# One 512-column matmul for both activation parts in the projections of a hybrid encoder trunk

## The chip, the cores and the metric

The kernel runs on one core of a Trainium2 chip. The metric is the device time of one execution in microseconds (us), given as the median of several runs; smaller is better. The engines are named as in the profile: PE is TensorE's matmul side, PEld its weight loads, DVE is VectorE, ACT is ScalarE, POOL is GpSimd and SP is SyncE, which issues the transfers.

## The reference

The reference is a two-layer encoder on 256 tokens of width 2048, in float32. Each layer normalises x, projects it to 6848 columns with one matrix, sends part of the columns through a recurrence in both directions over time (16 heads) and part through windowed attention (16 query heads, 4 key heads), gates both results, joins them and projects back to 2048 columns. Cut to what matters here:

```
for l in range(DEPTH):                                   # DEPTH = 2
    h = rms_norm(x, norm_g[l])
    proj = einsum('btd,dc->btc', h, w_in[l])             # 2048 -> 6848
    rw_in, g_rw, q, k_at, v_at, g_at = split(proj)
    rw_in = bidir_token_shift(rw_in, shift_mu[l])        # u + mu0*(prev-u) + mu1*(next-u)
    ...
    mix = concat([y_rw * silu(g_rw), y_at * silu(g_at)])
    x = x + einsum('btc,cd->btd', mix, w_out[l])         # 2048 -> 2048
return rms_norm(x, final_g)
```

The two large products, with `w_in` and `w_out`, are what the change touches.

## The kernel before, in words

**Precision by parts.** The matmuls of the projections read a rounded float32 form (`F32R`). To keep more of float32's accuracy each operand is split in a high part, the rounded value, and a low part, the rest. A product is then the sum of three matmuls: high weights by high activations, high weights by low activations, and low weights by high activations.

**Tiles and steps.** Activations lie transposed: 128 channels on the partitions, 16 such blocks, 256 tokens along the free dimension. A tile of an output is 128 columns of the projection by 256 tokens, accumulated in one PSUM tile `pm` over 16 steps of 128 input channels. One step (`gemm`, L292 to L294) is the three matmuls named above, each with its own load of 128x128 weights and 256 moving columns. Per layer there are 52 such input tiles: 42 are evacuated with a multiply by the norm `rb` (26 with the token shift, `shift_evac`, and 16 gates, `silu_evac`) and 10 are rotary (`rope_evac`). The output projection has 16 more (`queue_output`). The values of attention (`v_step`, L561 to L563) are the same three products with the activations as the stationary operand and 256 weight columns as the moving one, 32 steps a layer.

**Weights.** They stream in half tiles of 8 steps: one transfer of 512 KB to `raw` (three buffers), then `wsplit`, in two pieces of 512 columns: ACT writes `hi` (L222), DVE subtracts and writes `lo` (L224). `hi` and `lo` are separate tiles with two buffers each. The split of the next half tile is put into the program two steps before the present half tile ends (`PREFETCH`).

**Order.** PE runs in the order of the program (`manual_schedule` names PE alone). The order on DVE and ACT is set when the kernel is built, by a scheduler that goes by dependencies, priorities (`tc.high_priority`) and its own costs; instructions made with `PA` and `PV` keep program order among themselves. Each engine then works strictly through its list. A `Stream` holds the steps of all projections. `window` interleaves 64 steps, four tiles, with the pieces of the recurrence of several head pairs (`scan_p`, `scan_i`, `scan_b`, the yields of generators) in 14 slots, so that while ACT and DVE work on a piece of the recurrence, PE has steps to do. There are twelve such windows with recurrence work in each layer, then attention alone, then the 16 output tiles with nothing beside them. Once a window the recurrence takes a power on POOL (`yv`, L1000), between two instructions of DVE (L999 and the multiply into `ysq`).

**Evacuation.** When a tile's last matmul is done, DVE multiplies `pm` by `rb` into `u` or `g` (L434, L445), and ACT and DVE go on from there. Rotary tiles are copied out by ACT (L533). Output tiles are added to the residual by DVE (L624). `pm` has two buffers in `ps_main`, so PE can fill one tile while the other is evacuated. The split activations are `XH`, `XL` for the input and `MH`, `ML` for the output projection, each a buffer of 16 KB per partition in the pool `big`, which has four.

## Time and profile before

| | |
|---|---|
| time, median of 3 runs (lowest to highest) | 1187.89 us (1187.58 to 1188.18) |
| profiled execution, from the first to the last instruction | 1186.6 us |
| TensorE clock granted, mean | 0.995 |
| PE / PEld busy | 1160.9 us (98%) / 1082.7 us (91%) |
| DVE busy | 908.2 us (77%), 2017 instructions |
| ACT busy | 777.3 us (66%), 1955 instructions |
| matmuls | 16151 |
| moved to and from memory | 166.63 MB, mean 140 GB/s |

Rows of groups read: line, engine, operation, output <- inputs, shape, count; then the busy time in us and the mean of one in ns; then the idle time of the engine just before, and what ended it. In the timeline the first number is the start in us and the second what the instruction took. In the table by stage each engine has its busy time and, in brackets, its number of instructions; then come the granted clock of TensorE as a share, the share of the transfer engines and GB/s. Waits read: who waited for whom, total us, times, longest.

### The profile page before, as it was taken

The page shows a single profiled execution, that of the slowest core. Times are in us where ns is not written, and L with a number is a line of the kernel's source. Part 1 is how long each engine was busy: PE and PEld are TensorE (multiplying, and loading weights), DVE is VectorE, ACT ScalarE, POOL GpSimd, SP SyncE. Part 2 cuts the span into 40 slices and gives each one's busy share as a digit, 9 for nine tenths or more (in the row PEclk, how much of TensorE's full clock was granted, in tenths as well). Part 3 has the DMA queues.
Part 4 walks back from the last instruction along what each step waited for, and adds up shares of the span by engine and source line. Part 5 has one row for each costly group of instructions (what it writes and reads, how often), then busy time and mean ns, then how long its engine had stood idle before and what let it go on. Part 6 is the DMA issues. An engine that isn't in the chain of part 4 may idle for free.

```text
span 1186.6 us, 38095 instructions
## 1 busy us (share of the span) xinstructions
PE 1160.9 (98%) x16151; PEld 1082.7 (91%) x16151; DVE 908.2 (77%) x2017; ACT 777.3 (66%) x1955; POOL 18.7 (2%) x23
## 2 busy tenths in 40 slices
PE   8999999999999999999999999999999999999996
PEld 6988998999889989899999999999999998889996
DVE  6889878987877678766677988887887866786654
ACT  6666776777776666645555766876777666665553
POOL 0000000000000000000000000000000000000000
PEclk9999999999999999999999999999999999999998
DMA  7553333333323434477664443333323334345653
GB/s 257 164 170 123 109 107 116 108 98 115 109 94 122 136 117 142 134 234 236 210 184 165 134 131 114 95 113 117 122 83 109 122 124 132 114 145 190 213 185 123
DMA packets 60410, 166.63 MB, mean 140 GB/s; under 512 B 7728, under 2 KB 22736, under 8 KB 60240
## 3 DMA queue, kind: packets, MB, share of 16 engines
q1 hardware_dynamic: 60240, 164.21, 43.0%
q8 instruction: 126, 2.06, 0.7%
q14 instruction: 44, 0.36, 0.1%
HBM read 157.37 MB, written 4.19 MB: 136 GB/s over the span
## 4 chain that ended last, share of the span: by engine, by line
PE 74%; issue 15%; DVE 7%; ACT 2%; POOL 1%; DMA 1%; SPq 0%; DVEq 0%; POOLq 0%; ACTq 0%
PE pm L292 19%; PE pm L294 16%; PE pm L293 16%; PE pg L786 3%; DVE lo L224 2%; PE pcc L957 2%; PE py L987 2%; PE py L964 1%; PE pcc L980 1%; PE pq L899 1%; PE pcc L970 1%; PE pd L908 1%; PE pza L671 1%; POOL yv L1000 1%; PE pscr L1050 1%
## 5 line engine op out<-in xcount | busy, mean ns | idle before, releaser
L292 PE MATMUL pm<-XH,hi 128*128 128x256 f32 x1664 | 494.2, 297 | 3.9 <-ACT XH L184 1.6
L294 PE MATMUL pm<-XH,lo 128*128 128x256 f32 x1664 | 467.8, 281 | 5.9 <-DVE lo L224 5.8
L293 PE MATMUL pm<-XL,hi 128*128 128x256 f32 x1664 | 467.6, 281 | 0.8 <-DVE XL L185 0.6
L222 ACT ACTIVATE hi<-raw 128x512 fp32r<-128x512 f32 x560 | 328.2, 625 | 190.6 <-PE pm L293 91.8
L224 DVE TENSOR_TENSOR lo<-raw,hi 128x512 fp32r<-128x512 f32 x560 | 369.1, 686 | 102.5 <-ACT hi L222 95.2
L292 PEld LDWEIGHTS pm<-XH,hi 128*128 128x128 f32 x1664 | 313.4, 188 | 19.3 <-ACT XH L184 2.6
L294 PEld LDWEIGHTS pm<-XH,lo 128*128 128x128 f32 x1664 | 313.9, 189 | 8.3 <-DVE lo L224 8.3
L293 PEld LDWEIGHTS pm<-XL,hi 128*128 128x128 f32 x1664 | 314.1, 189 | 1.7 <-DVE XL L185 1.7
L292 PE MATMUL pm<-MH,hi 128*128 128x256 f32 x512 | 144.0, 281 | 0.0
L294 PE MATMUL pm<-MH,lo 128*128 128x256 f32 x512 | 143.8, 281 | 0.0
L293 PE MATMUL pm<-ML,hi 128*128 128x256 f32 x512 | 143.8, 281 | 0.0
L292 PEld LDWEIGHTS pm<-MH,hi 128*128 128x128 f32 x512 | 96.6, 189 | 0.8 <-issue 0.8
L293 PEld LDWEIGHTS pm<-ML,hi 128*128 128x128 f32 x512 | 96.6, 189 | 0.0
L294 PEld LDWEIGHTS pm<-MH,lo 128*128 128x128 f32 x512 | 96.6, 189 | 0.0
L910 DVE CAST_PREDICATED tv<-LV,pd 128x256 f16<-128x256 uint8 x80 | 34.2, 428 | 12.0 <-PE pd L908 11.4
L1065 ACT ACTIVATE mv<-mv,mx 128x257 f32<-128x257 f32 x64 | 31.9, 503 | 17.2 <-DVE mx L1062 17.2
L792 DVE TENSOR_TENSOR ge<-pg,C 128x1024 f32<-128x1024 f32 x32 | 38.8, 1219 | 2.3 <-PE pg L786 2.3
L975 ACT ACTIVATE suv<-pcc 64x128 f32<-64x128 f32 x128 | 34.3, 268 | 9.2 <-PE pcc L973 7.4
L959 ACT ACTIVATE rh<-pcc 128x128 f32<-128x128 f32 x64 | 17.5, 274 | 34.0 <-PE pcc L957 33.6
L902 ACT ACTIVATE QF<-pq 128x256 f16<-128x256 f32 x80 | 30.8, 384 | 12.5 <-PE pq L866 11.7
L786 PE MATMUL pg<-mv,bk 64*128 64x128 f32 x512 | 37.2, 285 | 0.3 <-DVE ge L792 0.3
L786 PEld LDWEIGHTS pg<-mv,bk 64*128 64x128 f32 x512 | 31.1, 187 | 2.4 <-DVE ge L792 0.4
(248 smaller groups left out, 1856.5 us busy)
## 6 DMA issues: line engine op xcount, KB each, us to landing
raw<-wi SPq DMA_DIRECT2D x207, 512.0 KB, 3.7
raw<-wo SPq DMA_DIRECT2D x64, 512.0 KB, 4.2
raw<-wv SPq DMA_DIRECT2D x8, 512.0 KB, 3.6
rrot<-u SPq DMA_DIRECT2D x80, 32.0 KB, 1.9
vg<-xT SPq DMA_DIRECT2D x16, 128.0 KB, 4.1
xd<-vg SPq DMA_DIRECT2D x16, 128.0 KB, 3.5
vg<-xd SPq DMA_DIRECT2D x16, 128.0 KB, 3.6
g<-dup SPq DMA_DIRECT2D x16, 97.0 KB
```

The lines of the kernel that those rows point to most:

```text
L222: A.activation(hi[:, q], raw[:, q], AF.Copy)
L224: V.tensor_tensor(lo[:, q], raw[:, q], hi[:, q].bitcast(F32), op=ALU.subtract)
L292: PE.matmul(pm, wh, rh[:, kk, :], start=(kk == 0), stop=False)
L293: PE.matmul(pm, wh, rl[:, kk, :], start=False, stop=False)
L294: PE.matmul(pm, wl, rh[:, kk, :], start=False, stop=(kk == 15))
L786: PE.matmul(pg[:, h, c * 128 : (c + 1) * 128], BK[half[h], d, c, 1 - h : 3 - h, :].rearrange("p s j -> p (s j)"), MV[half[h], d, c].rearra ...
L792: V.tensor_tensor(GEd(d), pg.rearrange("p h (c x) -> p h c x", c=NC), gm[d].unsqueeze(1).unsqueeze(1).to_broadcast([128, 2, NC, 128]), op= ...
L902: A.activation(t_sub(QF), flat4(pq[:, :, 0:128]), AF.Copy)
L910: V.copy_predicated(t_sub(TC), t_mask, flat4(pd[:, :, 0:128]))
L957: PE.matmul(pc[half[h], 0, d, :], GE[h][r, d, ci[d], 0, :], SUV[r, d, ci[d], h, :], start=True, stop=True)
L975: A.activation(here(h), pc[half[h], 1], AF.Copy)
L1065: A.activation(Sc[:, h, q, 0:257], Sc[:, h, q, 0:257], AF.Exp, scale=0.125, bias=mx[:, q : q + 1], accum_out=den[:, q : q + 1])
```

## The change

Both activation parts now lie beside each other in one buffer (`XP`, `MP`: 16 blocks, each of 256 high and 256 low columns), and both weight parts in one tile `hl`. A step has two matmuls: the high weights by 512 moving columns, both activation parts at once, into a PSUM tile of two halves; and the low weights by the 256 high columns into the first half. On a tile's last step the order of the two is turned round. The two halves, not yet one number, are added in the evacuation: in `joined` by a DVE `tensor_reduce` over pairs that are 256 elements apart, ahead of the multiply by `rb`; in the rotary tiles ACT copies the second half and DVE adds the first; in the output tiles a second DVE addition follows. `v_step` does the same with the two weight parts as 512 moving columns. The pool `big` has two buffers of twice the size.

```
-    big = pool("big", 4)
+    big = pool("big", 2)
...
+    def pairt(name):
+        hl = big.tile([128, NKT, 2, T], F32R, tag="big", name=name)
+        return hl, hl[:, :, 0], hl[:, :, 1]
...
     def wsplit(raw):
-        hi = wsp.tile([128, 1024], F32R, tag="hi", name="hi")
-        lo = wsp.tile([128, 1024], F32R, tag="lo", name="lo")
+        hl = wsp.tile([128, 2, 1024], F32R, tag="hl", name="hl")
+        hi, lo = hl[:, 0], hl[:, 1]
...
-        return hi, lo
+        return hi, lo, hl
...
-                    box.append(bank() if bank else ps_main.tile([128, T], F32, tag="m", name="pm"))
+                    box.append(bank() if bank else ps_main.tile([128, 2, T], F32, tag="m", name="pm"))
...
-                rh, rl = operands()
+                r = operands()
                 k = kk % 8
                 wh, wl = w[0][:, k * 128 : (k + 1) * 128], w[1][:, k * 128 : (k + 1) * 128]
-                PE.matmul(pm, wh, rh[:, kk, :], start=(kk == 0), stop=False)
-                PE.matmul(pm, wh, rl[:, kk, :], start=False, stop=False)
-                PE.matmul(pm, wl, rh[:, kk, :], start=False, stop=(kk == 15))
+
+                def high():
+                    PE.matmul(pm, wh, r[:, kk], start=(kk == 0), stop=(kk == 15), skip_group_check=True)
+
+                def low():
+                    PE.matmul(pm[:, 0], wl, r[:, kk, 0], start=False, stop=False, skip_group_check=True)
+
+                for part in (low, high) if kk == 15 else (high, low):
+                    part()
...
+        def joined(u, pm):
+            V.tensor_reduce(u, pm.rearrange("p s t -> p t s"), axis=AX.X, op=ALU.add)
+            V.tensor_tensor(u, u, L.norm.rb, op=ALU.mult)
...
-                V.tensor_tensor(u, pm, L.norm.rb, op=ALU.mult)
+                joined(u, pm)
...
-                V.tensor_tensor(g, pm, L.norm.rb, op=ALU.mult)
+                joined(g, pm)
...
-                A.activation(raw, pm, AF.Copy)
+                A.activation(raw, pm[:, 1], AF.Copy)
+                V.tensor_tensor(raw, pm[:, 0], raw, op=ALU.add)
...
-                wh, wl = (x[:, k * 256 : (k + 1) * 256] for x in w)
+                both = w[2][:, :, k * 256 : (k + 1) * 256]
                 tb = slice(b * 128, (b + 1) * 128)
-                PE.matmul(pvs[b], L.XH[:, kk, tb], wh, start=(kk == 0), stop=False)
-                PE.matmul(pvs[b], L.XH[:, kk, tb], wl, start=False, stop=False)
-                PE.matmul(pvs[b], L.XL[:, kk, tb], wh, start=False, stop=(kk == 15))
+                PE.matmul(pvs[b], L.XH[:, kk, tb], both, start=(kk == 0), stop=(kk == 15), skip_group_check=True)
+                PE.matmul(pvs[b][:, 0], L.XL[:, kk, tb], both[:, 0], start=False, stop=(kk == 15), skip_group_check=True)
...
-                A.activation(L.VA[:, 0, :], pvs[0], AF.Copy, scale=L.norm.rt[:, 0:1])
-                V.tensor_scalar(L.VA[:, 1, :], pvs[1], L.norm.rt[:, 1:2], None, op0=ALU.mult)
+                for b in range(2):
+                    A.activation(L.VA[:, b, :], pvs[b][:, 0], AF.Copy, scale=L.norm.rt[:, b : b + 1])
+                    V.scalar_tensor_tensor(
+                        L.VA[:, b, :], pvs[b][:, 1], L.norm.rt[:, b : b + 1], L.VA[:, b, :], op0=ALU.mult, op1=ALU.add
+                    )
...
-                V.tensor_tensor(x, pm, xs[0], op=ALU.add)
+                V.tensor_tensor(x, pm[:, 0], xs[0], op=ALU.add)
+                V.tensor_tensor(x, pm[:, 1], x, op=ALU.add)
```

The change moves instructions at three places. The first is PE's list at the first steps of the first tile, before (`XH`, `XL` are the activation parts, `hi`, `lo` the weight parts):

```order
L292 MATMUL pm<-XH,hi 128x256
L293 MATMUL pm<-XL,hi 128x256
L294 MATMUL pm<-XH,lo 128x256
L292 MATMUL pm<-XH,hi 128x256
L293 MATMUL pm<-XL,hi 128x256
L294 MATMUL pm<-XH,lo 128x256
```

and in the changed kernel at the end of the first tile and the start of the second (the line numbers have moved on):

```order
L299 MATMUL pm<-XP,hl 128x512
L302 MATMUL pm<-XP,hl 128x256
L299 MATMUL pm<-XP,hl 128x512
L302 MATMUL pm<-XP,hl 128x256 x2
L299 MATMUL pm<-XP,hl 128x512 x2
L302 MATMUL pm<-XP,hl 128x256
L299 MATMUL pm<-XP,hl 128x512
```

Three matmuls a step have become two; at the seam two of the short and two of the long follow each other. The second place is DVE's list around the power `yv` in a window of layer 1, before:

```order
L999 TENSOR_SCALAR yv<-yv 128x4
L237 TENSOR_TENSOR ysq<-py,yv 128x256
L224 TENSOR_TENSOR lo<-raw,hi 128x512 x2
L910 COPY_PREDICATED tv<-LV,pd 128x2x4x32
L237 TENSOR_TENSOR th<-lw,th 128x256
L445 TENSOR_TENSOR g<-pm,rb 128x256
L224 TENSOR_TENSOR lo<-raw,hi 128x512 x2
L447 SCALAR_TENSOR_TENSOR vg<-g 128x256
```

and in the changed kernel, where L229 writes the low weights, L930 is the former L910 and L443 and L444 are the reduce and the multiply:

```order
L1019 TENSOR_SCALAR yv<-yv 128x4
L453 SCALAR_TENSOR_TENSOR kr<-u,PR,kr 128x255
L242 TENSOR_TENSOR ysq<-py,yv 128x256
L229 TENSOR_TENSOR hl<-raw,hl 128x512
L930 COPY_PREDICATED tv<-LV,pd 128x2x4x32
L229 TENSOR_TENSOR hl<-raw,hl 128x512
L242 TENSOR_TENSOR th<-lw,th 128x256
L443 TENSOR_REDUCE g<-pm 128x256
L229 TENSOR_TENSOR hl<-raw,hl 128x512
L444 TENSOR_TENSOR g<-g,rb 128x256
L229 TENSOR_TENSOR hl<-raw,hl 128x512
```

The scheduler has put the last instruction of a token shift (L453) between the power's two DVE instructions, the copy into `tv` between the two low parts, and a low part between the reduce and its multiply. The third place is DVE's list in the output projection of layer 1, before:

```order
L624 TENSOR_TENSOR X_20063<-pm,vg 128x256
L224 TENSOR_TENSOR lo<-raw,hi 128x512 x2
L640 TENSOR_TENSOR acc<-acc,mf 128x256
L224 TENSOR_TENSOR lo<-raw,hi 128x512 x2
L624 TENSOR_TENSOR X_20063<-pm,vg 128x256
```

and changed:

```order
L643 TENSOR_TENSOR X_17932<-pm,vg 128x256
L644 TENSOR_TENSOR X_17932<-pm,X_17932 128x256
L229 TENSOR_TENSOR hl<-raw,hl 128x512 x2
L660 TENSOR_TENSOR acc<-acc,mf 128x256
L229 TENSOR_TENSOR hl<-raw,hl 128x512 x2
L643 TENSOR_TENSOR X_17932<-pm,vg 128x256
```

The order is the same but for the second addition behind the first.

More of the change, by code (lines that the diff above doesn't have):

```diff
@@ L479, in queue_inputs @@
         if l == 0:
-            inproj(0, lambda pm: S.later(29, lambda: xw_evac(pm)), raws=first_w, bank=lambda: wbank("pm")[:, 0:T])
+            inproj(0, lambda pm: S.later(29, lambda: xw_evac(pm)), raws=first_w, bank=lambda: wbank("pm").rearrange("p (s t) -> p s t", s=2))
             inproj(1, lambda pm: S.later(13, lambda: xa_evac(pm)))
@@ L556, in f @@
                 if not pvs:
-                    pvs.extend(ps_main.tile([128, T], F32, tag="m", name="pva") for _ in range(2))
+                    pvs.extend(ps_main.tile([128, 2, T], F32, tag="m", name="pva") for _ in range(2))
                 k = kk % 4
-                wh, wl = (x[:, k * 256 : (k + 1) * 256] for x in w)
+                both = w[2][:, :, k * 256 : (k + 1) * 256]
                 tb = slice(b * 128, (b + 1) * 128)
-                PE.matmul(pvs[b], L.XH[:, kk, tb], wh, start=(kk == 0), stop=False)
-                PE.matmul(pvs[b], L.XH[:, kk, tb], wl, start=False, stop=False)
-                PE.matmul(pvs[b], L.XL[:, kk, tb], wh, start=False, stop=(kk == 15))
+                PE.matmul(pvs[b], L.XH[:, kk, tb], both, start=(kk == 0), stop=(kk == 15), skip_group_check=True)
+                PE.matmul(pvs[b][:, 0], L.XL[:, kk, tb], both[:, 0], start=False, stop=(kk == 15), skip_group_check=True)
             return f
```

10 lines of the change are left out of this document (5 added, 5 removed).

## The prediction

> **What bounds the kernel now.** I read the page first: its busy rows and the engine line of the chain of waits.
>
> ```profile
> span 1186.6 us, 38095 instructions
> PE 1160.9 (98%) x16151; PEld 1082.7 (91%) x16151; DVE 908.2 (77%) x2017; ACT 777.3 (66%) x1955; POOL 18.7 (2%) x23
> ...
> PE 74%; issue 15%; DVE 7%; ACT 2%; POOL 1%; DMA 1%; SPq 0%; DVEq 0%; POOLq 0%; ACTq 0%
> ```
>
> TensorE (PE) ends almost every wait, and VectorE (DVE) is the only other engine with a share of the chain that matters. Since matmuls overlap, a busy PE says little about its pace. For that I read the table by stage: two full windows of layer 0's recurrence, two of layer 1's (each two POOL instructions long, since a window has one `yv` power), the two output projections, layer 0's attention, and then the two long stretches with recurrence work.
>
> ```profile
> core 0: us, PE busy (x) PEld busy (x) DVE busy (x) ACT busy (x) POOL busy (x), PEclk, DMA share, GB/s
> 189.85:272.82 82.97, 82.29 (x1502) 75.61 (x1502) 70.18 (x151) 60.08 (x162) 2.05 (x2) 1.00 0.34 108
> 770.34:852.70 82.36, 82.27 (x1502) 75.68 (x1501) 68.01 (x142) 59.81 (x162) 2.01 (x2) 1.00 0.34 109
> 504.30:595.20 90.90, 90.90 (x768) 90.90 (x767) 59.17 (x111) 47.26 (x95) 0.00 (x0) 1.00 0.72 227
> 1082.50:1173.40 90.90, 90.90 (x768) 90.90 (x767) 52.00 (x94) 47.72 (x93) 0.00 (x0) 1.00 0.59 186
> 440.00:504.30 64.30, 64.30 (x557) 58.52 (x553) 52.38 (x166) 43.63 (x120) 0.00 (x0) 1.00 0.45 144
> ...
> 51.00:440.00 389.00, 383.29 (x6433) 351.96 (x6433) 315.31 (x681) 271.73 (x711) 8.24 (x8) 1.00 0.36 116
> 632.00:1020.00 388.00, 384.72 (x6449) 353.89 (x6449) 310.20 (x662) 268.62 (x709) 8.06 (x8) 1.00 0.37 118
> ```
>
> The output projections are nothing but matmuls at full clock: 768 in 90.90 us is 118.4 ns each, 355.1 ns for the three of a step. The two layers' windows hold the same PE work (82.29 and 82.27 us), yet layer 0's take 41.49 us and layer 1's 41.18. DVE is busy 35.09 us of the one and 34.01 of the other. So DVE already leaks into the time: 1.08 us more of its work goes with 0.30 us more, 0.28 us per us.
>
> **TensorE.** These groups give the number of steps.
>
> ```profile
> L292 PE MATMUL pm<-XH,hi 128*128 128x256 f32 x1664 | 494.2, 297 | 3.9 <-ACT XH L184 1.6 <-ACT hi L222 1.4 <-DVE VA L571 0.7
> L292 PE MATMUL pm<-MH,hi 128*128 128x256 f32 x512 | 144.0, 281 | 0.0
> L561 PE MATMUL pva<-hi,XH 128*128 128x256 f32 x64 | 19.2, 300 | 0.0
> ```
>
> That is 1664 + 512 + 64 = 2240 steps. Each loses two matmuls of 256 columns and gets one of 512; the `lo` matmul stays at 118.4 ns. At the start some 30 steps wait for inputs (only 107 matmuls run in the first 24 us), so 2210 count.
>
> No f32 matmul of 512 columns is in the trace. From above, it costs two of the present: 236.8 ns, no gain. From below stand the f16 matmuls of the warm-up, whose last starts are 0.22 and 0.21 us apart at granted clock 1.00 (three overlapping views of the timeline, one row each, then the clock):
>
> ```profile
> 4.02 0.81 PE L1125 MATMUL warm<-QF 128*128 128x512 f16 x3
> 4.24 0.81 PE L1125 MATMUL warm<-QF 128*128 128x512 f16 x3
> 4.45 0.59 PE L1125 MATMUL warm<-QF 128*128 128x512 f16 x2
> ...
> 3.90:4.70 0.80, 0.80 (x6) 0.30 (x4) 0.63 (x1) 0.13 (x1) 0.00 (x0) 1.00 0.88 261
> ```
>
> So 215 ns for 512 columns, 0.42 ns a column, and 107.5 ns for 256: the present 118.4 carries 11 ns on top. Is that a fixed cost per matmul, or the weight load? The timeline shows the next load starting with each matmul, in lockstep with it:
>
> ```profile
> 1090.04 0.28 PE L292 MATMUL pm<-MH,hi 128*128 128x256 f32 x1
> 1090.04 0.19 PEld L293 LDWEIGHTS pm<-ML,hi 128*128 128x128 f32 x1
> 1090.15 0.28 PE L293 MATMUL pm<-ML,hi 128*128 128x256 f32 x1
> 1090.16 0.19 PEld L294 LDWEIGHTS pm<-MH,lo 128*128 128x128 f32 x1
> ```
>
> If the load sets the pace, the long matmul hides it and costs 215; if the 11 ns are fixed, 118.4 + 107.5 = 226. I take the middle, 221. A step is then 339 ns, 15.8 ns less: 2210 × 15.8 = **35 us off PE**. The ends are 0 (236.8) and, with 215 for the long one and 107.5 for the `lo` matmul too, 32.6 ns a step, 72 us.
>
> On the Trainium skill, TensorE: Matmul & The Clock Gate, section Back-to-back issue gap, gives N/2.4 + 2.5 ns, 109 ns for 256 columns and 216 for 512. The trace's 118.4 does not agree with the first; by the rule for both, a step would be 325 ns and the gain 30 ns a step, about 66 us.
>
> **VectorE.** The cost of an instruction is the distance of starts, since neighbours overlap (first rows of the timeline, then groups).
>
> ```profile
> 224.81 0.68 DVE L224 TENSOR_TENSOR lo<-raw,hi 128x512 fp32r<-128x512 f32 x1
> 225.41 0.68 DVE L237 TENSOR_TENSOR bk<-lw,ip 128x512 f32<-128x512 f32 x1
> ...
> 229.78 0.42 DVE L237 TENSOR_TENSOR lw<-lw 128x256 f32<-128x256 f32 x1
> 230.11 0.69 DVE L224 TENSOR_TENSOR lo<-raw,hi 128x512 fp32r<-128x512 f32 x1
> ...
> L434 DVE TENSOR_TENSOR u<-pm,rb 128x256 f32<-128x256 f32 x52 | 21.1, 408 | 10.0 <-PE pm L294 9.9
> L445 DVE TENSOR_TENSOR g<-pm,rb 128x256 f32<-128x256 f32 x32 | 13.4, 418 | 5.2 <-PE pm L294 5.2
> L792 DVE TENSOR_TENSOR ge<-pg,C 128x1024 f32<-128x1024 f32 x32 | 38.8, 1219 | 2.3 <-PE pg L786 2.3
> ```
>
> 512 elements cost 0.60 us, 256 cost 0.33, and a PSUM source costs no more (408 to 418 ns against 420 for `lw`). The multiply by `rb` remains in all 52 + 32 = 84 evacuations, so what is added is the reduce. It reads 512 elements and writes 256; from below, priced by its output, 0.33 us; from above, were a read that jumps 1 KB each time half as fast, the 1024 elements of L792 with the same overlap, 1.14. I take 0.60, the row with the same number of inputs. That is 84 × 0.60 = 50 us more DVE, with 20 additions for the rotary tiles and 32 for the output tiles (52 × 0.33 = 17 us) 67 us in all; `v_evac` adds two instructions per layer. The ACT copy of the rotary tiles stays, at half the tile.
>
> What hides it: a window has four evacuations, 2.4 us. DVE goes from 34.0 to 36.4 us in layer 1 and from 35.1 to 37.5 in layer 0, in windows that PE alone would shorten by 64 × 15.8 ns = 1.0 us, to 40.2 and 40.5. That is 91% and 93%. If this cover were gone, all 2.4 us would be on the path. At the slope above, 2.4 us more work and 1.0 us less room cost (2.4 + 1.0) × 0.28 = 0.95 us a window. The stretches with recurrence work, 389 + 388 us, are 18.8 windows: **18 us given back**. What is late then is `lo`: the reduce waits for PE as L434 does now, and behind it in DVE's queue stand the next `lo`, which PE's 256-column matmul needs, and `tv`, which the recurrence's matmuls need.
>
> Each attention stage (DVE 52.38 of 64.30 us) holds 8 tiles, by the order in the code six gates and two rotary: 6 × 0.60 + 2 × 0.33 = 4.3 us more, in 128 steps that are 2.0 us shorter. At the slope, 1.8 us each, 3.6. In the output projections DVE has 31 us free of 90.90, so 16 × 0.33 us is hidden; only the last tile's addition shows, 0.4 us at each end, 0.8.
>
> **Edits at nothing.** One `hl` tile for both weight parts comes free after its last matmul, where `hi` came free one earlier: ACT's `hi` starts up to 118 ns later, before work that is due a half tile (8 steps, 2.7 us) on. `v_step` needs `lo` with its first matmul, 8 loads in all. Two large buffers in place of four hold the same bytes in the same order. `pm` fills a bank but still has two buffers, and comes free with the reduce, 16 steps before it is wanted. SP's transfers stay the same.
>
> **The sum**, against the profiled 1186.6: −35 + 18 + 3.6 + 0.8 gives 1174.0. The median of the runs, 1187.89, is 1.3 above the span, so I add 1.3: **1175 us**.
>
> **Rivals.** (a) *The weight load was the pace and DVE finds room.* For it: the lockstep, and that some DVE waits are for PE and shrink; against it: DVE at over 90%. The long matmul costs 215, a step 333.4, 21.7 ns less: 48 us gained; with a third of the payback (7): 1187.9 − 48 + 7 = 1147. The page's 325 ns would take it to about 1135.
>
> (b) *The long matmul costs two short ones.* Nothing in the trace excludes it, though the f16 rows speak against it. PE gains nothing; DVE costs 2.4 × 0.28 × 18.8 = 13 us, and 3 us in attention and at the ends: 1204, slower. This side begins where the gain falls under some 17 us, at 8 ns a step, so from 229 ns for the long matmul.
>
> (c) *The reduce is slow and DVE becomes the bound.* At 1.14 us, four add 4.6 us: 38.6 and 39.7 us of work a window. These waits of one window of layer 1 (797 to 838 us) follow DVE's own results through POOL and ACT, and do not shrink:
>
> ```profile
> DVE ysq L237 <- POOL yv L1000: 1.2, 1, 1.2
> DVE t L237 <- ACT t L1009: 1.1, 1, 1.1
> ...
> DVE tt L894 <- ACT AB L237: 0.6, 1, 0.6
> ```
>
> With their 2.9 us a window takes 41.5 and 42.6, on average 0.7 more than now: +13 us over 18.8. The output projections still gain 512 × 15.8 ns = 8 us, attention and the start perhaps 2: 1191, slower. For it: no row reads PSUM with a stride. Against it: nothing on DVE runs at that rate but the reciprocal and the scan.
> The Trainium skill, Advanced Engine Details and Errata, section PSUM Cachelines, says that every two consecutive elements should be contiguous, for matmuls; the reduce's pairs lie 1 KB apart. No run here shows what DVE makes of that.
>
> **How the numbers follow.** The forecast has 0.48, with its own range 1156 to 1184; (a) 0.27, (b) 0.11, (c) 0.14. Under 1140 lies a part of (a), above 1199 most of (b): the range is 1140 to 1199. 0.2% is 2.4 us, about what a measurement of this kernel tells from no change. Faster: nearly all of the forecast and of (a), 0.74. Slower: (b) and two thirds of (c), 0.20. Same: the rest, 0.06.
>
> **What would show it.** In the output projections 256 steps take 90.90 us; 86.8 confirms 339 ns a step, 85.4 speaks for 215 ns, 90.9 for (b). The reduce's row should read near 0.68 us, or 1.2 for (c). Windows between two `yv` powers should take about 41.1; 40.2 means that DVE has room, over 42 that it is the bound. Waits of PE for `lo` or `tv` (L224 and L910 of before) should grow with DVE's load. The forecast is wrong if the step's price is off by more than 5 ns, or if DVE's payback is not linear in its load.

## The result: 1.0% slower

The changed kernel takes **1200.04 us** (median of 4 runs, 1196.87 to 1201.83) beside 1187.74 us for the kernel before in the same session (1187.35 to 1188.18): a ratio of 1.0098, 95% interval [1.0083, 1.0113]. The prediction was 1175 us, range 1140 to 1199, so both the number and the sign were wrong. The profiled execution of the changed kernel took 1200.67 us with a span of 1198.9, against 1186.6 before; the working below goes by spans. In the changed kernel's four runs the time goes with the mean granted clock: 0.993 in the shortest (1196.87), 0.987 in the longest (1201.83).

The page of the changed kernel, the same rows as the prediction showed of before:

```profile
span 1198.9 us, 33727 instructions
PE 1155.1 (96%) x13911; PEld 958.5 (80%) x13911; DVE 973.7 (81%) x2155; ACT 780.0 (65%) x1957; POOL 21.5 (2%) x23
...
PE 52%; DVE 22%; issue 17%; ACT 5%; DMA 3%; POOL 1%; SPq 0%; DVEq 0%; POOLq 0%; ACTq 0%
```

The 2240 matmuls are gone from PE (16151 to 13911), and DVE has 65.5 us more work (908.2 to 973.7). What is new is in the chain: DVE ends 22% of it, where it was 7%, and PE 52%, where it was 74%. The groups with what ended the idle time before them, of the changed kernel:

```profile
L299 PE MATMUL pm<-XP,hl 128*128 128x512 f32 x1664 | 621.7, 412 | 8.1 <-DVE XP L190 2.8 <-DVE VA L588 2.7 <-ACT hl L227 2.6
L302 PE MATMUL pm<-XP,hl 128*128 128x256 f32 x1664 | 452.2, 282 | 8.2 <-DVE hl L229 8.2
...
L443 DVE TENSOR_REDUCE u<-pm 128x256 f32<-128x512 f32 x52 | 35.0, 675 | 7.5 <-PE pm L299 7.2
```

and of the kernel before the three rows that answer the first two:

```profile
L292 PE MATMUL pm<-XH,hi 128*128 128x256 f32 x1664 | 494.2, 297 | 3.9 <-ACT XH L184 1.6 <-ACT hi L222 1.4 <-DVE VA L571 0.7
L294 PE MATMUL pm<-XH,lo 128*128 128x256 f32 x1664 | 467.8, 281 | 5.9 <-DVE lo L224 5.8
L293 PE MATMUL pm<-XL,hi 128*128 128x256 f32 x1664 | 467.6, 281 | 0.8 <-DVE XL L185 0.6
```

The reduce takes 0.675 us. PE's own idle time ahead of the projections' matmuls goes from 10.6 to 16.3 us (3.9 + 5.9 + 0.8 against 8.1 + 8.2), and the waits that grew are for `VA` (0.7 to 2.7), for the high weights (1.4 to 2.6) and for the low weights (5.8 to 8.2). The wait that grew most stands elsewhere. The recurrence's matmuls `pg` wait until DVE has made the product `ge` from their PSUM tile; first the row of the changed kernel, then that of before:

```profile
L806 PE MATMUL pg<-mv,bk 64*128 64x128 f32 x512 | 37.2, 285 | 5.5 <-DVE ge L812 5.5
...
L786 PE MATMUL pg<-mv,bk 64*128 64x128 f32 x512 | 37.2, 285 | 0.3 <-DVE ge L792 0.3
```

Two more matmuls of the recurrence, `pbn` and `pt`, wait 2.2 us each behind `ge` in the changed kernel and not at all before.

**The price of the long matmul** is read in the output projection, where PE waits for nothing (timeline of PE, changed kernel; start, duration, ...):

```profile
1099.94 0.39 PE L299 MATMUL pm<-MP,hl 128*128 128x512 f32 x1
1100.16 0.28 PE L302 MATMUL pm<-MP,hl 128*128 128x256 f32 x1
1100.28 0.39 PE L299 MATMUL pm<-MP,hl 128*128 128x512 f32 x1
1100.51 0.28 PE L302 MATMUL pm<-MP,hl 128*128 128x256 f32 x1
1100.63 0.39 PE L299 MATMUL pm<-MP,hl 128*128 128x512 f32 x1
```

From the long one's start to the short one's it is 0.22 to 0.23 us; over the stage the mean is 230 ns, and 117 back. A step is 347 ns where it was 355.1: **8 ns saved, not 15.8**.

**By stage** (the columns are those of the prediction's table). Of the changed kernel: layer 0's window with the largest loss, a window of layer 1, layer 1's output projection, and 3.4 us from the first of these:

```profile
core 0: us, PE busy (x) PEld busy (x) DVE busy (x) ACT busy (x) POOL busy (x), PEclk, DMA share, GB/s
324.30:369.40 45.10, 42.35 (x688) 35.02 (x687) 32.54 (x66) 30.97 (x82) 1.01 (x1) 0.96 0.28 97
...
866.50:907.40 40.90, 40.51 (x687) 33.69 (x686) 36.26 (x76) 30.24 (x82) 1.08 (x1) 1.00 0.33 109
...
1095.00:1184.50 89.50, 89.50 (x518) 78.32 (x518) 58.45 (x111) 48.77 (x94) 0.00 (x0) 1.00 0.59 194
...
354.40:357.80 3.40, 3.40 (x32) 2.77 (x32) 2.73 (x5) 0.25 (x1) 0.00 (x0) 0.50 0.06 22
```

Before, the first two were:

```profile
314.60:356.80 42.20, 41.12 (x752) 37.70 (x751) 31.26 (x63) 30.84 (x81) 0.96 (x1) 1.00 0.33 106
...
852.70:893.90 41.20, 41.17 (x752) 37.88 (x752) 34.02 (x71) 29.94 (x82) 1.03 (x2) 1.00 0.33 109
```

The window of layer 1 has become 0.3 us shorter, with DVE busy for 36.26 of its 40.90 us. The window of layer 0 has become 2.9 us longer, though DVE has hardly more to do in it than before (32.54 for 31.26). So the loss is not where DVE is fullest. Also, for 3.4 us of that window TensorE was granted half its clock.

The starts of the `yv` powers on POOL, one a window, give such a comparison for the whole program. Three of them in the changed kernel:

```profile
279.16 1.71 POOL L1020 TENSOR_TENSOR yv<-yv,mhalf 128x4 f32<-128x4 f32 x1 [39.96 <-DVE yv L1019]
324.31 1.01 POOL L1020 TENSOR_TENSOR yv<-yv,mhalf 128x4 f32<-128x4 f32 x1 [43.44 <-DVE yv L1019]
369.44 1.01 POOL L1020 TENSOR_TENSOR yv<-yv,mhalf 128x4 f32<-128x4 f32 x1 [44.12 <-DVE yv L1019]
```

and the same three before:

```profile
272.82 1.04 POOL L1000 TENSOR_TENSOR yv<-yv,mhalf 128x4 f32<-128x4 f32 x1 [40.40 <-DVE yv L999]
314.56 1.01 POOL L1000 TENSOR_TENSOR yv<-yv,mhalf 128x4 f32<-128x4 f32 x1 [40.69 <-DVE yv L999]
356.81 1.01 POOL L1000 TENSOR_TENSOR yv<-yv,mhalf 128x4 f32<-128x4 f32 x1 [41.24 <-DVE yv L999]
```

The first pair is 45.15 us apart, where it was 41.74: 3.4 us more; the second 45.13 for 42.25. In this way, with the norm's powers between the layers, the span is cut into stages. The table gives what each takes before, and how much longer (+) or shorter it is in the changed kernel and in four of the experiments below (us, one profiled execution each):

| stage | before | changed | no joining | joining alone | earlier split | three remedies |
|---|---|---|---|---|---|---|
| start to 1st power of layer 0 | 148.3 | +5.4 | −1.1 | +3.7 | +2.1 | +1.0 |
| powers 1 to 4 | 124.5 | +1.0 | −3.0 | +1.6 | −1.0 | −2.0 |
| 4 to 5 | 41.7 | +3.4 | 0.0 | +0.8 | +0.7 | +0.3 |
| 5 to 6 | 42.3 | +2.9 | +0.1 | +3.1 | +1.2 | +0.5 |
| 6 to 8 | 76.2 | −0.9 | −0.8 | +0.4 | −0.8 | −0.9 |
| attention, output of layer 0 | 165.9 | +0.1 | −3.8 | +1.8 | −0.2 | −0.8 |
| start of layer 1 to 1st power | 130.3 | +2.6 | −1.3 | +3.8 | +0.2 | −0.3 |
| powers 1 to 6 | 206.0 | −0.7 | −2.6 | +2.8 | +2.5 | −1.7 |
| 6 to 8 | 76.2 | −0.7 | −0.8 | +0.5 | −0.8 | −0.8 |
| attention, output of layer 1 | 164.4 | −1.3 | −3.6 | +1.5 | −0.9 | −1.0 |
| end | 10.9 | +0.5 | 0.0 | +0.2 | 0.0 | 0.0 |
| span | 1186.6 | +12.3 | −16.7 | +20.0 | +2.7 | −5.8 |

Four stages of the changed kernel, the starts of both layers and two windows of layer 0, hold 14.3 us of loss, more than the whole 12.3.

**What stands at these places.** At the sixth power of layer 0 the values of attention end. `v_evac` now needs DVE for both of its halves (L588), and they stand in DVE's list behind a reciprocal. DVE and PE in the changed kernel:

```profile
350.73 1.76 DVE L242 RECIPROCAL kd<-pk 128x256 f32<-128x256 f32 x1
...
353.53 0.87 DVE L588 SCALAR_TENSOR_TENSOR VA<-pva,rt,VA 128x256 f32<-128x256 f32 x2
...
354.06 0.54 PE L299 MATMUL pm<-XP,hl 128*128 128x512 f32 x1 [1.96 <-DVE VA L588]
...
354.40 0.41 PE L302 MATMUL pm<-XP,hl 128*128 128x256 f32 x1
...
354.62 0.63 PE L299 MATMUL pm<-XP,hl 128*128 128x512 f32 x1
```

and before, where ACT did the one half and DVE one instruction (L571) for the other:

```profile
340.69 1.76 DVE L237 RECIPROCAL kd<-pk 128x256 f32<-128x256 f32 x1
...
342.37 0.39 DVE L571 TENSOR_SCALAR VA<-pva,rt 128x256 f32<-128x256 f32 x1
...
342.81 0.38 PE L292 MATMUL pm<-XH,hi 128*128 128x256 f32 x1 [0.66 <-DVE VA L571]
```

Both PSUM buffers of `ps_main` hold the values until then, so PE has no tile to fill, and its pause is 1.96 us in place of 0.66. Behind it the matmuls take 0.41 and 0.63 us instead of 0.28 and 0.39: that is the stretch of 3.4 us at granted clock 0.50 in the table of stages. At half speed, 3.4 us do the work of 1.7. The changed kernel's profile has four such stretches between its start and its end (at 84.7, 313.4, 354.4 and 675.2 us), the kernel before none. They make some 4 × 1.7 = **6.8 us** of the 12.3, by this estimate; run 7 below gives a measured price. Each follows a pause or two of PE. At 84.7 and 675.2, in the starts of the layers, PE stood 1.1 us and then 1.1 us again, released both times by DVE's `ge` (1.21 us each), where the kernel before has no such wait. At 313.4 the split of the weights by ACT was late. ACT and PE in the changed kernel:

```profile
306.23 1.28 ACT L242 ACT_TABLE_LOAD   x1
...
311.60 0.41 ACT L242 ACTIVATE duh<-g 97x256 fp32r<-97x256 f32 x1
311.90 2.18 ACT L227 ACTIVATE hl<-raw 128x512 fp32r<-128x512 f32 x4
```

and before, where the next high part stands ahead of four other instructions:

```profile
299.25 1.28 ACT L237 ACT_TABLE_LOAD   x1
...
303.20 0.63 ACT L222 ACTIVATE hi<-raw 128x512 fp32r<-128x512 f32 x1
303.86 0.38 ACT L902 ACTIVATE QF<-pq 128x256 f16<-128x256 f32 x1
```

From the table load of the rotary sine to the next high part it was 4.0 us, and is 5.7 now.

### The profile page after: what moved, and what is told of

Same layout as the page of the kernel before. It is cut to its first block, busy times and chain, and to the rows that moved or that the text cites. A ratio compares the mean times of both kernels' runs of the same rounds, so it can differ in the third digit from the quotient of the medians.

```text
span 1198.9 us, 33727 instructions
## 1 busy us (share of the span) xinstructions
PE 1155.1 (96%) x13911; PEld 958.5 (80%) x13911; DVE 973.7 (81%) x2155; ACT 780.0 (65%) x1957; POOL 21.5 (2%) x23
## 4 chain that ended last, share of the span: by engine, by line
PE 52%; DVE 22%; issue 17%; ACT 5%; DMA 3%; POOL 1%; SPq 0%; DVEq 0%; POOLq 0%; ACTq 0%
PE pm L299 24%; PE pm L302 11%; DVE hl L229 7%; ACT hl L227 2%; DVE kd L242 2%; DVE lw L242 2%; DVE ge L812 2%; PE pg L806 1%; PE py L984 1%; PE pcc L1000 1%; DMA raw<-wi 1%; PE pcc L990 1%; PE pcc L977 1%; PE py L1007 1%; DVE tv L930 1%
## 5 line engine op out<-in xcount | busy, mean ns | idle before, releaser
L299 PE MATMUL pm<-XP,hl 128*128 128x512 f32 x1664 | 621.7, 412 | 8.1 <-DVE XP L190 2.8
L302 PE MATMUL pm<-XP,hl 128*128 128x256 f32 x1664 | 452.2, 282 | 8.2 <-DVE hl L229 8.2
L227 ACT ACTIVATE hl<-raw 128x512 fp32r<-128x512 f32 x560 | 325.2, 624 | 192.4 <-issue 58.1
L229 DVE TENSOR_TENSOR hl<-raw,hl 128x512 fp32r<-128x512 f32 x560 | 371.0, 685 | 60.4 <-ACT hl L227 57.5
L299 PEld LDWEIGHTS pm<-XP,hl 128*128 128x128 f32 x1664 | 310.2, 189 | 77.0 <-DVE XP L190 4.7
L302 PEld LDWEIGHTS pm<-XP,hl 128*128 128x128 f32 x1664 | 315.8, 190 | 20.2 <-DVE hl L229 13.1
L299 PE MATMUL pm<-MP,hl 128*128 128x512 f32 x512 | 176.3, 393 | 0.8 <-ACT hl L227 0.8
L302 PE MATMUL pm<-MP,hl 128*128 128x256 f32 x512 | 138.2, 280 | 0.4 <-DVE hl L229 0.2
L299 PEld LDWEIGHTS pm<-MP,hl 128*128 128x128 f32 x512 | 94.0, 188 | 20.6 <-ACT hl L227 1.1
L302 PEld LDWEIGHTS pm<-MP,hl 128*128 128x128 f32 x512 | 96.2, 188 | 3.6 <-DVE hl L229 1.0
L1085 ACT ACTIVATE mv<-mv,mx 128x257 f32<-128x257 f32 x64 | 31.9, 503 | 14.4 <-DVE mx L1082 14.3
L443 DVE TENSOR_REDUCE u<-pm 128x256 f32<-128x512 f32 x52 | 35.0, 675 | 7.5 <-PE pm L299 7.2
L979 ACT ACTIVATE rh<-pcc 128x128 f32<-128x128 f32 x64 | 17.5, 273 | 34.2 <-PE pcc L977 33.9
L930 DVE CAST_PREDICATED tv<-LV,pd 128x256 f16<-128x256 uint8 x80 | 34.0, 425 | 6.2 <-PE pd L928 6.0
L451 ACT ACTIVATE kr<-u,DP 128x256 f32<-128x256 f32 x36 | 18.2, 509 | 21.9 <-DVE u L444 21.8
L1002 DVE TENSOR_TENSOR suv<-pcc,pc 64x128 f32<-64x128 f32 x96 | 27.5, 286 | 6.1 <-PE pcc L1000 5.2
```

Of the source, the lines that this page charges most:

```text
L227: A.activation(hi[:, q], raw[:, q], AF.Copy)
L229: V.tensor_tensor(lo[:, q], raw[:, q], hi[:, q].bitcast(F32), op=ALU.subtract)
L299: PE.matmul(pm, wh, r[:, kk], start=(kk == 0), stop=(kk == 15), skip_group_check=True)
L302: PE.matmul(pm[:, 0], wl, r[:, kk, 0], start=False, stop=False, skip_group_check=True)
L443: V.tensor_reduce(u, pm.rearrange("p s t -> p t s"), axis=AX.X, op=ALU.add)
L930: V.copy_predicated(t_sub(TC), t_mask, flat4(pd[:, :, 0:128]))
```

## The experiments

**Theory A**: the long matmul saves 8 ns a step, some 19 us, and DVE's added work takes some 31 us back, as waits of PE. **Rival B**: the loss lies in what else the change brought, the joint buffers and tiles and the order of the matmuls. Three runs tell these apart, and a fourth gives the output projection alone.

**1. The new matmuls without the joining.** The evacuations of before read only the first half of each tile. The second half, high weights by low activations, is computed and left out of the result.

```
-            V.tensor_reduce(u, pm.rearrange("p s t -> p t s"), axis=AX.X, op=ALU.add)
-            V.tensor_tensor(u, u, L.norm.rb, op=ALU.mult)
+            V.tensor_tensor(u, pm[:, 0], L.norm.rb, op=ALU.mult)
...
-                A.activation(raw, pm[:, 1], AF.Copy)
-                V.tensor_tensor(raw, pm[:, 0], raw, op=ALU.add)
+                A.activation(raw, pm[:, 0], AF.Copy)
...
-                V.tensor_tensor(x, pm[:, 1], x, op=ALU.add)
```

> The changed kernel's matmuls with the evacuations of before: only the first half of each PSUM tile is read, so the high weights' product with the low activations (and the high activations' with the low weights of the values) is left out of the result. Theory A (PE gains 8 ns a step, 230 ns for the long matmul in place of 2 x 118, and DVE's extra work costs some 31 us): 1188 - 2240 x 8.4 ns = 1169 us, within 3, no stretch at half clock between 20 and 1170 us, and no PE gap above 1.4 us after the start. Theory B (the loss comes from the layout: one tile for both weight parts, full-bank PSUM tiles, paired activations): 1185 us or more, and the gaps stay.

Measured: **1170.85 us** (1169.83 to 1172.91), ratio 0.9859 [0.9845, 0.9874]. Its page:

```profile
PE 1143.6 (98%) x13911; PEld 953.5 (81%) x13911; DVE 908.5 (78%) x2017; ACT 774.9 (66%) x1955; POOL 18.7 (2%) x23
```

The whole new arrangement of matmuls, buffers and tiles, with DVE's work as before (908.5 us), gains 16.7 us of span, spread over the stages as the steps are (the table's third column). Rival B falls: the layout costs nothing that shows. No half-clock stretch stands between this run's start and end.

**2. The joining without the new matmuls.** Three matmuls of 256 columns again, two of them into the one half and the other half, and the changed kernel's evacuations.

```
-                    PE.matmul(pm, wh, r[:, kk], start=(kk == 0), stop=(kk == 15), skip_group_check=True)
+                    PE.matmul(pm[:, 0], wh, r[:, kk, 0], start=(kk == 0), stop=False, skip_group_check=True)
+                    PE.matmul(pm[:, 1], wh, r[:, kk, 1], start=False, stop=(kk == 15), skip_group_check=True)
```

> Three matmuls of 256 columns a step as before, but the high weights' product with the low activations goes to the second half of the PSUM tile, and all evacuations are those of the changed kernel. Theory A: no gain on PE and DVE's full extra work, with 8 ns a step more room than in the changed kernel: 1198 to 1213 us. Theory C (DVE's extra work hurts only because PE runs faster): 1190 us or less.

Measured: **1207.58 us** (1203.87 to 1208.4), ratio 1.0160 [1.0142, 1.0178]. With PE as slow as before, the joining costs 20.0 us of span. On top of run 1 it costs 29.0 (1169.9 to 1198.9). So the two parts of the change do not add up: −16.7 and +20.0 would be +3, and +12.3 is measured. Of the 9 us between them some 5 are half-clock stretches, one here (after the values, at 350 us) and four in the changed kernel; that the rest is DVE's work in windows that a faster PE has shortened is argued, not shown.

**3. ACT takes over a part of the joining.** For the 84 tiles that used the reduce, ACT copies the second half and DVE adds 256 elements.

```
-            V.tensor_reduce(u, pm.rearrange("p s t -> p t s"), axis=AX.X, op=ALU.add)
+            A.activation(u, pm[:, 1], AF.Copy)
+            V.tensor_tensor(u, pm[:, 0], u, op=ALU.add)
```

> The changed kernel, but in the 84 evacuations ACT copies the second half out of PSUM and DVE adds the first half to it (256 elements) in place of the 512-element reduce: 0.27 us less DVE work and 0.37 us more ACT work each. Theory A: the payback falls with DVE's extra work, 45 us in place of 67: 1180 to 1192 us. Theory B: 1200 us as the changed kernel. If the time gets longer, it is the hop from ACT to DVE, not DVE's load, that is late.

Measured: **1188.92 us** (1188.09 to 1191.91), ratio 1.0011 [1.0001, 1.0020]. The groups that replace the reduce's 0.675 us:

```profile
L444 DVE TENSOR_TENSOR u<-pm,u 128x256 f32<-128x256 f32 x52 | 21.4, 411 | 19.5 <-ACT u L443 19.4
...
L443 ACT ACTIVATE u<-pm 128x256 f32<-128x256 f32 x52 | 19.8, 381 | 13.2 <-PE pm L299 12.6
```

DVE goes down by 18.2 us (973.7 to 955.5) and ACT up by 22.3, and the time falls by 11 us. So the added hop from ACT to DVE costs less than the DVE time that it saves, and ACT has room for the copy. How much of the 11 us is DVE's time and how much the new order of its list, this run does not separate; two of the four half-clock stretches are gone as well. The loss at the start of layer 0 goes from +5.4 to +0.7 and at the start of layer 1 from +2.6 to +0.4. The two windows of layer 0 keep theirs (+3.2, +2.7), each with a half-clock stretch: these are not a matter of the reduce.

**4. Only the output projections changed.** All tiles of the input projection and the values as before; the 32 output tiles with the long matmul.

```
+                if not wide:
+                    PE.matmul(pm, wh, r[:, kk, 0], start=(kk == 0), stop=False)
+                    PE.matmul(pm, wh, r[:, kk, 1], start=False, stop=False)
+                    PE.matmul(pm, wl, r[:, kk, 0], start=False, stop=(kk == 15))
+                    return
...
+            gemm(wo[l, k], lambda: L.MP, ev, begin=be, wide=True)
```

> The change in the output projection alone (32 tiles, 512 steps), where DVE has a third of its time free; the input projections and the values keep three matmuls of 256 columns and the evacuations of before, on the paired layout. Theory A: 512 x 8.4 ns = 4.3 us less, 0.8 back at the ends: 1184 us, faster than both kernels. Theory B: 1190 us or more, since the layout stays.

Measured: **1184.75 us** (1183.57 to 1185.04), ratio 0.9973 [0.9961, 0.9984]: faster than both kernels. Where PE sets the pace alone and DVE has room, the change gives what its matmuls save: 1.8 us in each of the two stages.

**5 and 6. Where the long matmul's price comes from.** Both start from run 4. In the one, steps 2 to 15 of the output projection use 64 of the 128 weight columns; in the other the long matmul has 384 columns instead of 512 (the low activations by half). Both leave that part of the product out.

```
+                    n = 64 if 0 < kk < 15 else 128
+                    PE.matmul(pm[0:n], wh[:, 0:n], r[:, kk], start=(kk == 0), stop=(kk == 15), skip_group_check=True)
...
+                    PE.matmul(pm[0:n, 0], wl[:, 0:n], r[:, kk, 0], start=False, stop=False, skip_group_check=True)
```

```
+                    n = 384 if 0 < kk < 15 else 512
+                    PE.matmul(pm.rearrange("p s t -> p (s t)")[:, 0:n], wh, r[:, kk].rearrange("p s t -> p (s t)")[:, 0:n], start=(kk == 0), stop=(kk == 15), skip_group_check=True)
```

> Only the output projection is changed (two matmuls a step), and its steps 1 to 14 use 64 of the 128 weight columns, so half of the output channels lack most of their sum; a weight load is half as long. It measures what sets the pace of 230 ns (512 columns) and 117 ns (256). If the load of 128 weights sets the pace of the short matmul: 109 ns after a short one; if loading slows the stream of the long one: 216 to 220 ns in place of 230. If the price is the stream's own (0.436 ns a column and 7 ns): 230 and 117 as with 128 weights.

> Only the output projection is changed, and the long matmul of steps 1 to 14 has 384 columns in place of 512: half of the high weights' product with the low activations is left out. If the price goes by columns throughout (118 at 256, 230 at 512): 174 ns. If the weight load sets the floor at 256 columns and the stream runs at 0.417 ns a column: 177 ns. If a long matmul has a cost of its own: nearer 185.

Measured: 1185.21 and 1166.06 us (one execution each). The weight loads of run 5, a row of the groups:

```profile
L306 PEld LDWEIGHTS pm<-MP,hl 128*64 128x64 f32 x448 | 60.1, 134 | 41.9
```

its timeline of PE:

```profile
1099.94 0.39 PE L306 MATMUL pm<-MP,hl 128*64 128x512 f32 x1
1100.17 0.28 PE L310 MATMUL pm<-MP,hl 128*64 128x256 f32 x1
1100.28 0.39 PE L306 MATMUL pm<-MP,hl 128*64 128x512 f32 x1
```

and that of run 6:

```profile
1099.87 0.34 PE L306 MATMUL pm<-MP,hl 128*128 128x384 f32 x1
1100.04 0.28 PE L309 MATMUL pm<-MP,hl 128*128 128x256 f32 x1
1100.16 0.34 PE L306 MATMUL pm<-MP,hl 128*128 128x384 f32 x1
```

The half load takes 134 ns instead of 188, and the pace stays 0.23 and 0.11: the load is not what sets it. With 384 columns the long matmul takes 0.17 to 0.18 us. So the price goes by columns: 118 ns for 256, about 175 for 384, 230 for 512, that is 0.44 ns a column with some 7 ns fixed. Merging two matmuls of 256 saves one fixed part and nothing else: 2 × 118.4 − 230 = 7 ns.

**7. The values of attention as before.** Everything else is the changed kernel.

```
-                for b in range(2):
-                    A.activation(L.VA[:, b, :], pvs[b][:, 0], AF.Copy, scale=L.norm.rt[:, b : b + 1])
-                    V.scalar_tensor_tensor(
-                        L.VA[:, b, :], pvs[b][:, 1], L.norm.rt[:, b : b + 1], L.VA[:, b, :], op0=ALU.mult, op1=ALU.add
-                    )
+                A.activation(L.VA[:, 0, :], pvs[0], AF.Copy, scale=L.norm.rt[:, 0:1])
+                V.tensor_scalar(L.VA[:, 1, :], pvs[1], L.norm.rt[:, 1:2], None, op0=ALU.mult)
```

> The changed kernel with the values of attention as before: three matmuls of 256 columns a step and one instruction for each half of the evacuation, one on ACT and one on DVE. Theory A (both PSUM buffers of the projections stay taken until DVE, behind a reciprocal, has finished the values, and the pause brings 3.4 us at half clock): the stage between the fifth and sixth power of layer 0 falls from 45.1 to 42.6 us, the clock stretch at 354 us is gone, and the time falls by 3 us, 0.5 lost on PE, to 1197 us. Theory D (that stage is long from DVE's load alone): 44.5 us or more there, 1200 us.

Measured: **1194.16 us** (1193.01 to 1196.12), ratio 1.0055 [1.0039, 1.0072]; 6 us less than the changed kernel. The window of the values is back to +0.2 us from +2.9, and the stretch behind it is gone. The rest of the 6 us is chance in part: the pauses before 84.7 and 313.4 us are still there in this execution, of the same length, and no half clock follows them (the one in the start of layer 1 remains). This pair of executions also prices a stretch: without it the start of layer 0 is 2.2 us shorter than in the changed kernel and the window between its fourth and fifth power 1.4 us, on either side of the 1.7 worked out above, while the three windows between agree within 0.1 us.

**8. Selected tiles.** Run 4, with the long matmul also in the tiles 34 to 43 of layer 0's input projection and 10 to 43 of layer 1's, joined with ACT's help as in run 3.

```
+WIDE = (range(34, 44), range(10, 44))
...
-            gemm(wi[l, ct], lambda: L.XP, evac, **kw)
+            gemm(wi[l, ct], lambda: L.XP, evac, wide=ct in WIDE[l], **kw)
```

> Two matmuls a step in the output projection, and in input tiles away from the dense stretches: 34 to 43 in layer 0 and 10 to 43 in layer 1, with the halves joined with ACT's help; the other tiles and the values as before. Theory A (DVE's added work costs only where DVE has no room): 1184.7 less 0.9 in layer 0 and 1.8 in layer 1: 1182 us. Theory E (any joining beside the recurrence costs what it gains): 1184 to 1188 us.

Measured: **1182.36 us** (1181.59 to 1182.82), ratio 0.9951 [0.9936, 0.9965], as theory A said and below theory E's range.

**9 to 11. The weights are split earlier.** The stages that lose most have PE waiting for a weight part. If these were queued too late, a longer lead would help the changed kernel (9), and not the kernel before (10, the control). Run 11 is run 8 with the same edit.

```
-PREFETCH = 2
+PREFETCH = 4
```

> The changed kernel, whose weight tiles are split into their two parts when four steps of the tile before are left, where it were two. If the 31 us that VectorE gives back are mostly stretches in which TensorE waits for a weight part that was queued too late (theory A1), some 0.7 us more lead covers a third or more of them: 1187 to 1193, with fewer than the three half-clock stretches outside the ends. If they come from the order of the values' path and of the recurrence's chain (theory A2), the lead changes nothing: 1197 to 1203.

> The control: the kernel before with the same earlier split. It has no such stretches, so both theories expect no change, 1186 to 1190; a gain or a loss here would have to be taken off the run of the changed kernel with the same edit.

> The selected tiles (1182.4) with the earlier split. A1 expects a part of what is left in the windows back, 1178 to 1181; A2 1182, as without it.

Measured: 9, **1191.44 us** (1190.84 to 1192.07), ratio 1.0031 [1.0018, 1.0044]; 10, **1184.71 us**, ratio 0.9975 [0.9964, 0.9985]; 11, **1180.33 us** (1179.44 to 1180.75), ratio 0.9937 [0.9922, 0.9952].

The changed kernel gets 8.6 us back, but the control, for which both theories expected nothing, gains 3.1. That leaves 5.5 us, a sixth of the 31, where A1 asked for a third. So the late split is a part of it and not the bulk. The part may be the half-clock stretches: this execution has none between start and end (mean clock 0.996 against 0.988), and 5.5 is near the 6.8 us that the four cost. That is argued from one execution. The other four took the same time with 0.992 to 0.993, which doesn't tell: run 5 reads 0.993 without any stretch in mid-program, from half clock at its start and end alone. The remaining loss has also moved: the starts of both layers and layer 0's windows are better by 3.3, 2.4 and 6.4 us (powers 1 to 6 of layer 0: 2.0, 2.7, 1.7), and the five windows of layer 1 are worse by 3.2. The pause at the values is as long as ever, as A2 said. PE's timeline in run 9 at this place:

```profile
345.85 0.51 PE L299 MATMUL pm<-XP,hl 128*128 128x512 f32 x1 [2.06 <-DVE VA L588]
```

and the table of stages for the 3.4 us from there:

```profile
345.80:349.20 3.40, 3.35 (x64) 2.86 (x65) 3.12 (x6) 1.30 (x5) 0.00 (x0) 1.00 0.02 5
```

Here PE paused 2.06 us, and 64 matmuls, small ones among them, followed in 3.4 us at full clock. In the changed kernel a pause of 1.96 us was followed by 32 in 3.4 us, at half.

**12. Three remedies together**, with the long matmul in all tiles: the values as in run 7, ACT's copy as in run 3, the earlier split as in run 9.

> All tiles keep the long matmul; three things together that the earlier runs tried alone: the values of attention as before, ScalarE copies the second half of each tile and VectorE adds 256 elements in place of the reduce, and the weights are split four steps ahead. If what VectorE's added work costs lies in these few places, the savings add up: 1200.0 less 11 (the copy) less 3 (the values' pause without its half-clock stretch) less 3 to 6 (the split) gives 1180 to 1183, level with the selected tiles. If the three remedies cover the same waits, the sum is not reached: 1185 to 1189, no better than the copy alone.

Measured: **1183.42 us** (1182.36 to 1185.91), ratio 0.9965 [0.9955, 0.9974], just above the 1180 to 1183 of savings that add up and well under 1185. Alone, however, they took 11.1, 5.9 and 8.6 us off the changed kernel, 25.6 together, and here it is 16.6. The 9 us of overlap look like stretches counted twice: the profiled executions of runs 3, 7 and 9 lack two, three and all four of the four, nine in all or some 15 us, and this one lacks three (one is left at 83.1 us), some 5 us. Apart from the clock, then, the savings add up within about 1 us, so the three remedies seem to cover different waits. Of the 29.0 us that the joining cost on top of run 1, 10.9 are left (1180.8 for 1169.9). But the earlier split gives 3.1 us of this to the kernel before as well, against whose 1184.71 this version gains 1.3 us (not compared in one session).

## Why the prediction was wrong

**The size of the long matmul, the failed step.** "I take the middle, 221": it costs 230 ns, 4 ns above the 226 that the prediction gave for a fixed cost. The lockstep of loads and matmuls had been half of the argument, and run 5 shows that the load has no part in the pace. The other half, the f16 rows with 0.42 ns a column, is nearly right for float32 (0.44). The 11 ns taken as fixed were partly a higher price per column, which the long matmul pays twice. The gain is 2210 × 8.4 = 18.6 us by the pace, and 16.7 in run 1, not 35. The check that the prediction named says so: 256 steps at 347 to 348 ns are 89 us, between its 86.8 and the 90.9 of rival (b). The Trainium skill, TensorE: Matmul & The Clock Gate, section Back-to-back issue gap, gives N/2.4 + 2.5 ns for a warm matmul; 109, 163 and 216 ns by it stand against the measured 118, 175 and 230, and the 66 us that the prediction worked out from it is four times what run 1 measured. (With 66 in place of 48, rival (a)'s sum is 1187.9 − 66 + 7 = 1129, not the 1135 given; nothing else hangs on it.)

**With 230 ns the prediction's own working gives no change.** A window is then only 0.54 us shorter on PE: (2.4 + 0.54) × 0.28 × 18.8 = 15.5 us back, in attention (4.3 + 1.08) × 0.28 × 2 = 3.0, at the ends 0.8. That is −18.6 + 19.3 = +0.7, a span of 1187.3. That agrees with the prediction's own rule for the sign, by which rival (b) begins at 229 ns for the long matmul; the measured +12.3 is far beyond what this rule gives at 230. The price alone thus explains 13 of the 25 us between the predicted span of 1174.0 and the measured 1198.9.

**The payback was taken as linear, and that failed too.** Its other 12 us: 1.9 of gain that run 1 lacks, and 29.0 us of payback (run 1 to the changed kernel) instead of 19.3. The slope of 0.28 us per us came from two plain windows. For these it holds or overstates: with all of the joining in them, the windows of layer 1 became 0.1 us shorter on average (powers 1 to 6, −0.7), when the slope asked for 0.3 more each. But the loss is at places the slope doesn't see, where an instruction that PE waits for falls behind a long one on DVE or ACT. Of the 29.0 us, 17.5 are time in which PE stands idle (span less PE's busy time: 26.3 us in run 1, 43.8 in the changed kernel). The waits that grew most are for DVE's `ge` (2.3 to 9.9 us), the low weights (5.5 to 8.5), `VA` (0.7 to 2.7) and, on ACT, the high weights (1.6 to 3.4). The prediction had named `lo` and `tv`, not `ge`. The largest part of the 9.7 us between 29.0 and 19.3 is the clock, some 6.8 us, in which PE counts as busy. The prediction never asked what TensorE's clock does when PE pauses.

**"Edits at nothing" held an edit that cost some 3 us.** Of `v_evac` it said only that it adds two instructions per layer. What mattered is whom they keep waiting: both PSUM buffers are held until DVE has come to them. Run 7 shows the price, 2.7 us in layer 0's window of the values, of which some 1.7 are the half clock behind the pause, already counted above.

**What was right.** The reduce at "near 0.68 us" (0.675; a stride of 1 KB in PSUM costs nothing, and rival (c) falls). The Trainium skill, VectorE: DVE Perf Modes, section The perf-mode tier table, allows `tensor_reduce` only the plain rate, from PSUM too; the reduce's row agrees, since it takes as long as the prediction's 0.68 us for 512 elements in SBUF. DVE's added work: 67 us predicted, 65.5 measured. The second addition in the output projections is hidden (run 4). The joint tile, the larger buffers and the merged `hl` cost nothing that run 1 shows. That PE's waits for `lo` should grow (5.8 to 8.2 us in the groups), and the sentence that the forecast fails "if the step's price is off by more than 5 ns, or if DVE's payback is not linear": both came about.

**What stays open.** Some 22 of the 29 us are left without the clock, most of them the waits for DVE named above. No run separates waits for want of DVE's time from waits made by the scheduler's new order, since each edit to the one moves the other: run 9 took 12 us from the starts and layer 0's windows and gave 3.2 back in layer 1's. Why the same edit gains 3.1 us in the kernel before was not followed up; of its 2.4 us of span, 1.2 lie in the start of layer 1 and 1.0 in the five windows behind it.

## What to carry to other kernels

Merging two matmuls into a longer one saves one fixed part, here 7 ns of 237, not half of the price; measure that part by the price at two lengths in the data type itself. Work that is moved from PE to a second engine is paid where PE waits for that engine, so look first for the places where the second engine's list stands between PE and its next buffer, and apply the change only where there is none (run 11: 1180.33 us, ratio 0.9937 [0.9922, 0.9952], the best version found). When PE is the bound, count a pause of one and a half to two microseconds as able to cost some 1.7 us more behind it.

## What was unexpected in the hardware

- **Half clock after short pauses.** In the changed kernel the granted clock is about half for 3.4 us after PE's pauses: 1.62 us before 313.4 us, 2.14 before 354.4, and 1.4 + 1.5 us in a row before 84.7 and before 675.2 (from one matmul's start to the next). The same pauses need not lead to it: not 2.23 us in run 9, not 1.62 in run 7. Where a pause falls matters. The four stretches begin 228.70, 40.96 and 320.85 us apart, which is 67, 12 and 94 times 3.413 us, and each lasts 3.41 us. So the clock is set on a grid of such cells. The traces of all fourteen kernels, between 20 us and the last output tile, were divided into these cells, laid out from where half clock sets in at each program's end. All six cells in which PE was idle for 1.8 us or more are followed by one cell at half clock, four of the six with 1.4 to 1.65 us are, and none with 1.35 or less. The pause of run 9 is cut by a border into 0.40 and 1.65 us. At the very end of two programs 1.1 us was enough, so idle time is not the whole rule, and what decides between 1.4 and 1.65 us stays open. The Trainium skill, TensorE: Matmul & The Clock Gate, section on the HAM clock gate, gives half rate after at least one idle window of about 3.4 us, in windows that run free of the kernel. The stretch's length and the chance in it agree; that the pause has to fill a window does not, since none of these was longer than 2.3 us.
- **A spread of runs that the kernel may make itself.** The kernel before stays within 0.8 us over the four runs beside the changed one, and spreads over 3.6 in sixteen others (1186.66 to 1190.24); the changed one spreads over 5.0 in four, with mean clock 0.993 at its shortest and 0.987 at its longest. Three stretches more or less of 1.7 us each would be that much. That their number varies was seen between profiled executions of different kernels alone, so this cause of the spread is not shown.
- **The load of half the weight columns** takes 134 ns instead of 188 and changes nothing in the pace (run 5).
